# Low halves of two weight blocks per pair: GpSimd subtraction replaced by a ScalarE negation and an accumulating transfer

## The chip, the cores and the metric

The kernel runs on one core of one Trainium2 chip. The metric is the device time of one execution in microseconds (us). The kernel before takes 930.64 us, the median of 3 runs (930.52 to 931.39).

## The reference

One decoder layer over 512 tokens of width 1024, in float32: a SwiGLU feed-forward layer, a mixer (dilated attention beside a diagonal state-space model), and a second SwiGLU layer. Each sub-layer is wrapped in RMS norms and added to the residual.

```
def swiglu(x, w_in, w_out):
    gate, up = jnp.split(x @ w_in, 2, axis=-1)
    return (jax.nn.silu(gate) * up) @ w_out

    h = rms_norm(x, ffn1_pre_g[l])
    x = x + 0.5 * rms_norm(swiglu(h, ffn1_w_in[l], ffn1_w_out[l]), ffn1_post_g[l])
    ...
    h = rms_norm(x, ffn2_pre_g[l])
    x = x + 0.5 * rms_norm(swiglu(h, ffn2_w_in[l], ffn2_w_out[l]), ffn2_post_g[l])
```

`w_in` is 1024 x 5632 (2816 gate and 2816 up columns), `w_out` is 2816 x 1024. The change touches only the two `w_in` products.

## The kernel before

**Split products.** TensorE works on a reduced float32 format (fp32r). To keep float32 accuracy each operand is split into a high half, which is the value rounded to fp32r, and a low half, which is the value minus its high half. A product is then three matmuls: high times high, high times low of the activations, low times high of the weights (`mm3`, lines 136 to 139, and `times`, lines 570 to 577).

**Weights.** A weight block of 128 x 1024 float32 (512 KB) is fetched by a DMA that SyncE issues (`block`, line 559, `load`, line 109). ScalarE writes the high half `whi` (line 105), and VectorE or, where `pool=True`, GpSimd writes the low half `wlo` (line 107). `whi` and `wlo` each have four buffers for the whole kernel, used in rotation. So the cut of a block can begin when TensorE has finished with the block four cuts earlier.

**Pairs.** The first blocks of hidden columns are done in the plain way, eight in the first layer and six in the second. The rest of each `w_in` product is done two column blocks at a time by a scheme of seven block products in place of eight (`seven`, lines 494 to 627). One call of `pair(f)` loads four raw blocks, a11 and a12 (gate columns, tile `wraw`, three buffers) and a21 and a22 (up columns, tile `wx`, three buffers). It forms three sums on VectorE (c3 = a11 + a21, c2 = c3 + a22, c1 = a21 + a22, and later c2 + a12, tile `wsum`), cuts seven blocks into halves (a11, a12, c2, c1, c3, the second c2, a22) and multiplies each with a prepared block of activations, 24 matmuls of 128 x 256 per cut. The sums of products stay in three PSUM banks, X (`wx` in the rows of TensorE), Y (`wy`) and Q (`wq`). ScalarE copies X away twice and Q once in between (`keep`, line 579), since the same bank goes on accumulating in the next product. Of the seven cuts, five have their low half made by VectorE, and two, a12 and a22, by GpSimd.

There are 15 pairs: 7 in the first feed-forward layer (f = 8 to 20) and 8 in the second (f = 6 to 20). Output products `outp` stand between some of them, after f = 12 in the first layer and after f = 10 and f = 16 in the second. So the pairs come in five unbroken runs.

**Order of work.** All matmuls are kept in the order of the program (`fix`, line 123). The instructions of the pairs on ScalarE, VectorE, GpSimd and SyncE have no such order written: a planner places them on each engine by its own costs, and each engine then runs its list in order. A DMA is issued by an engine's queue when its turn comes and its waits are met. No DMA of the kernel before is issued by GpSimd.

Of the kernel before, what the change touches and what calls it, by code (L numbers as in the profile page):

```python
# [8 lines left out]
F32 = mybir.dt.float32  # L9
F32R = mybir.dt.float32r  # L10
I32 = mybir.dt.int32
AF = mybir.ActivationFunctionType
ALU = mybir.AluOpType
# [30 lines left out]
class Layer:  # L44
# [449 lines left out]
    def seven(self, fin, w_in, ig, r, ah, al):  # L494
# [4 lines left out]
        nc, V = self.nc, self.nc.vector  # L499
# [64 lines left out]

        def cut(t, pool=False):
            hi, lo = (self.wp.tile([P, 1024], F32R, name=n, tag=n, bufs=4) for n in ("whi", "wlo"))
            self.wsplit(t, hi, lo, pool)
            return hi, lo

        def times(bank, w, xb, first):  # L570
# [13 lines left out]
        def pair(f, late=False):  # L584
# [5 lines left out]
            X = self.bank("wx")  # L590
            a11 = block(f, 0, 0)
            times(X, cut(a11), b11, True)
            s1 = keep(X)
            a12 = block(f, 0, 1)
            h12 = cut(a12, True)
            Y = self.bank("wy")
            times(Y, h12, b21, True)
# [4 lines left out]
            c2 = wsum()  # L602
            add(c3, a22, c2)
            times(X, cut(c2), n2, False)
            s2 = keep(X)
            c1 = wsum()
# [873 lines left out]
```

## Time and profile before

| | |
|---|---|
| median of 3 runs | 930.64 us |
| the profiled execution | 929.2 us, of which the span from its first to its last instruction is 927.4 us |
| granted TensorE clock | 0.999 of full speed |
| TensorE busy | 99% of the span |
| VectorE, ScalarE, GpSimd busy | 70%, 48%, 23% |
| low halves of a12 and a22 on GpSimd | 30 of GpSimd's 127 instructions |

In the rows, PE is TensorE (PEld its weight loads), DVE is VectorE, ACT is ScalarE, POOL is GpSimd and SP is SyncE. A row of a timeline has the start in us, the duration in us, the engine, the line of the kernel, the operation, and what is written from what, then the idle time before it and what ended that. A row of a tile's view has shortest, median and longest duration in ns, and the first and last start in us.

### The profile page before, as it was taken

What the parts mean: (1) busy time and instruction counts of PE and PEld (TensorE: products, weight loads), DVE (VectorE), ACT (ScalarE), POOL (GpSimd) and SP (SyncE); (2) the same over time, 40 slices, a digit from 0 to 9 for tenths busy, and PEclk for the clock granted to TensorE, in tenths of its full rate; (3) what the DMA queues carried; (4) which work ended last, traced back from release to release, by engine and by line L of the source; (5) the groups of instructions that cost most, each with busy time, mean ns of one, the idle gap of its engine ahead of it and who ended that gap; (6) DMA issues with size and microseconds to landing.
All of it is one profiled execution on the core that took longest, in us unless ns stands there. A gap on an engine that the chain in (4) does not pass through costs nothing.

```text
span 927.4 us, 15348 instructions
## 1 busy us (share of the span) xinstructions
PE 914.6 (99%) x6162; PEld 817.6 (88%) x6162; DVE 650.2 (70%) x1071; ACT 442.6 (48%) x685; POOL 213.7 (23%) x127
## 2 busy tenths in 40 slices
PE   9999999999999999999999999999999999999996
PEld 7887789998999989978777899888899989998995
DVE  6999694755577566758898568698367556755856
ACT  7263764552355443525745654482355414541542
POOL 0433202222223134500000025432122312231321
PEclk9999999999999999999999999999999999999999
DMA  8224652324231162283321440345223322332322
GB/s 274 91 69 139 213 207 90 110 84 132 84 117 44 58 195 90 88 207 122 114 69 56 162 148 24 84 167 182 92 93 113 114 92 94 112 114 93 94 88 90
DMA packets 47590, 106.81 MB, mean 115 GB/s; under 512 B 7808, under 2 KB 11136, under 8 KB 46976
## 3 DMA queue, kind: packets, MB, share of 16 engines
q1 hardware_dynamic: 45936, 102.21, 34.0%
q10 hardware_dynamic: 1584, 3.63, 1.1%
q8 instruction: 48, 0.79, 0.3%
q14 instruction: 22, 0.18, 0.1%
HBM read 96.13 MB, written 9.70 MB: 114 GB/s over the span
## 4 chain that ended last, share of the span: by engine, by line
PE 82%; DVE 3%; DMA 2%; issue 1%; ACT 1%; POOLq 0%; POOL 0%; DVEq 0%; SPq 0%; ACTq 0%
PE yo L132 21%; PE wx L132 18%; PE wq L132 9%; PE yt L132 6%; PE gu L132 5%; PE first L132 5%; PE wy L132 5%; PE prj L132 4%; PE prv L132 2%; PE mo L132 2%; PE st L132 1%; PE ys L132 1%; DMA w1d<-w1s 1%; PE pt L1070 1%; PE sc L132 1%
## 5 line engine op out<-in xcount | busy, mean ns | idle before, releaser
L105 ACT CAST whi<-wraw 128x1024 fp32r<-128x1024 f32 (+5 forms) x129 | 125.1, 977 | 164.3 <-PE yo L132 65.5
L107 POOL TENSOR_TENSOR wlo<-wraw,whi 128x1024 fp32r<-128x1024 f32 (+1 forms) x41 | 109.3, 2665 | 305.0 <-ACT whi L105 297.7
L107 DVE TENSOR_TENSOR wlo<-wraw,whi 128x1024 fp32r<-128x1024 f32 (+5 forms) x88 | 106.9, 1222 | 87.6 <-ACT whi L105 87.4
L132 PE MATMUL wx<-tq,whi 128*128 128x256 f32 x720 | 129.3, 280 | 0.0
L132 PEld LDWEIGHTS wx<-tq,whi 128*128 128x128 f32 x720 | 110.3, 188 | 0.0
L107 DVE TENSOR_TENSOR wlo<-wsum,whi 128x1024 fp32r<-128x1024 f32 x60 | 73.3, 1221 | 46.7 <-ACT whi L105 46.7
L105 ACT CAST whi<-wsum 128x1024 fp32r<-128x1024 f32 x60 | 62.9, 1049 | 90.2 <-PE yo L132 28.0
L132 PE MATMUL wx<-tq,wlo 128*128 128x256 f32 x360 | 100.4, 279 | 0.0
L107 POOL TENSOR_TENSOR wlo<-wx,whi 128x1024 fp32r<-128x1024 f32 x15 | 39.1, 2608 | 185.1 <-ACT whi L105 185.1
L132 PE MATMUL gu<-xh,wlo 128*128 128x512 f32 x176 | 69.0, 392 | 1.9 <-POOL wlo L107 1.2
L132 PE MATMUL gu<-xh,whi 128*128 128x512 f32 x176 | 70.6, 401 | 0.0
L132 PE MATMUL gu<-xl,whi 128*128 128x512 f32 x176 | 68.6, 390 | 0.0
L132 PE MATMUL wq<-bh,wlo 128*128 128x256 f32 x240 | 68.1, 284 | 0.0
L132 PE MATMUL wq<-bh,whi 128*128 128x256 f32 x240 | 68.0, 283 | 0.0
L132 PE MATMUL wq<-bl,whi 128*128 128x256 f32 x240 | 67.9, 283 | 0.0
L132 PEld LDWEIGHTS wx<-tq,wlo 128*128 128x128 f32 x360 | 67.6, 188 | 0.0
L132 PE MATMUL yo<-ah,whi 128*128 128x512 f32 x144 | 56.3, 391 | 0.0
L132 PE MATMUL yo<-whi,ah 128*128 128x512 f32 x144 | 56.1, 389 | 0.0
L132 PE MATMUL yo<-ah,wlo 128*128 128x512 f32 x144 | 56.1, 389 | 0.0
L132 PE MATMUL yo<-al,whi 128*128 128x512 f32 x144 | 56.0, 389 | 0.0
L132 PE MATMUL yo<-whi,al 128*128 128x512 f32 x144 | 56.0, 389 | 0.0
L132 PE MATMUL yo<-wlo,ah 128*128 128x512 f32 x144 | 56.0, 389 | 0.0
(261 smaller groups left out, 2384.8 us busy)
## 6 DMA issues: line engine op xcount, KB each, us to landing
wraw<-w1i SPq DMA_DIRECT2D x28, 512.0 KB, 3.6
wraw<-w2i SPq DMA_DIRECT2D x28, 512.0 KB, 3.6
wraw<-w2o SPq DMA_DIRECT2D x18, 512.0 KB, 3.8
wx<-w2i SPq DMA_DIRECT2D x16, 512.0 KB, 3.7
wx<-w1i SPq DMA_DIRECT2D x14, 512.0 KB, 3.6
wraw<-wmi SPq DMA_DIRECT2D x12, 512.0 KB, 3.8
wraw<-w1o SPq DMA_DIRECT2D x8, 512.0 KB, 4.3
wraw<-w1o SPq DMA_DIRECT2D x8, 384.0 KB, 3.0
```

Of the source, the lines that this page charges most:

```text
L105: fix(self.nc.scalar.copy(out=hi, in_=raw))
L107: fix(eng.tensor_tensor(out=lo, in0=raw, in1=hi.bitcast(F32), op=ALU.subtract))
L132: i = self.nc.tensor.matmul(*a, **k)
L1070: self.fix(nc.tensor.transpose(b[i][:, o:o + P], sc[:, c:c + P], self.ident))
```

## The change

Inside a pair, the two cuts that were made with GpSimd no longer use `wsplit`. ScalarE still writes the high half. ScalarE then also writes the negative of the high half into the low half's buffer, and a transfer issued by GpSimd adds the raw block to what stands there. The value is the same: raw minus high. All other cuts, in the pairs and outside, stay as they are.

```
--- before.py
+++ after.py
@@ -564,7 +564,12 @@

         def cut(t, pool=False):
             hi, lo = (self.wp.tile([P, 1024], F32R, name=n, tag=n, bufs=4) for n in ("whi", "wlo"))
-            self.wsplit(t, hi, lo, pool)
+            if pool:
+                nc.scalar.copy(out=hi, in_=t)
+                nc.scalar.activation(out=lo, in_=hi.bitcast(F32), func=AF.Copy, scale=-1.0)
+                nc.gpsimd.dma_start(out=lo, in_=t, accum_op=ALU.add)
+            else:
+                self.wsplit(t, hi, lo)
             return hi, lo
```

The two calls with `pool=True` are `cut(a12, True)` (line 595) and `cut(a22, True)` (line 617).

## The prediction

> **What bounds the kernel now.** I began with the page, then asked what waits for the 30 low halves that the change moves, and last read one pair on every engine.
>
> ```profile
> span 927.4 us, 15348 instructions
> ...
> PE 914.6 (99%) x6162; PEld 817.6 (88%) x6162; DVE 650.2 (70%) x1071; ACT 442.6 (48%) x685; POOL 213.7 (23%) x127
> ```
>
> TensorE is busy for 914.6 of 927.4 us. Nothing that frees another engine can gain more than the 12.8 us between them, and only where TensorE waits for what is freed. The view of the low halves that GpSimd writes tells whether it does:
>
> ```profile
> L107 POOL TENSOR_TENSOR wlo<-wraw,whi x41: 1844/2406/6822, 24.1 to 893.8; 128x1024 fp32r<-128x1024 f32 x37, 128x768 fp32r<-128x768 f32 x4
> L107 POOL TENSOR_TENSOR wlo<-wx,whi x15: 2427/2437/3061, 159.3 to 888.1; 128x1024 fp32r<-128x1024 f32 x15
> ...
>   ACT whi L105: 482.7, 51
> ...
> who waited for it (us, times):
>   PEld gu L132: 1.6, 1
>   PE gu L132: 1.2, 1
> ```
>
> The waits of TensorE on these tiles are one on a weight load and one on a matmul, both of `gu`, a bank of the plain products. No product of a pair (`wx`, `wy`, `wq`) waited for GpSimd even once. So the change takes nothing off the path. It can only keep the time or add to it, and the question is how much room the new chain has. One pair lasts 20.0 us, and TensorE does not stop in it:
>
> ```profile
> core 0: us, PE busy (x) PEld busy (x) DVE busy (x) ACT busy (x) POOL busy (x), PEclk, DMA share, GB/s
> 169.44:189.46 20.02, 20.02 (x171) 20.02 (x170) 14.85 (x16) 10.74 (x12) 5.42 (x2) 1.00 0.28 92
> ```
>
> **The room.** In the timelines of the first layer's second pair, a22 (`wx`) is cut from 158.13 and a12 of the next pair (`wraw`) from 163.80:
>
> ```profile
> 158.13 1.05 ACT L105 CAST whi<-wx 128x1024 fp32r<-128x1024 f32 x1 [1.78 <-PE wx L132]
> 159.09 0.58 ACT L581 COPY kp<-wx 128x512 f32<-128x512 f32 x1
> 160.97 1.05 ACT L105 CAST whi<-wraw 128x1024 fp32r<-128x1024 f32 x1 [1.30 <-PE wq L132]
> 161.93 0.57 ACT L581 COPY kp<-wq 128x512 f32<-128x512 f32 x1
> 163.80 1.05 ACT L105 CAST whi<-wraw 128x1024 fp32r<-128x1024 f32 x1 [1.30 <-PE wx L132]
> 166.69 1.05 ACT L105 CAST whi<-wsum 128x1024 fp32r<-128x1024 f32 x1 [1.83 <-PE wq L132]
> ```
> ```profile
> 159.26 2.44 POOL L107 TENSOR_TENSOR wlo<-wx,whi 128x1024 fp32r<-128x1024 f32 x1 [17.12 <-ACT whi L105]
> 164.93 2.40 POOL L107 TENSOR_TENSOR wlo<-wraw,whi 128x1024 fp32r<-128x1024 f32 x1 [3.23 <-ACT whi L105]
> ```
> ```profile
> 160.89 0.40 PE L132 MATMUL wx<-tq,whi 128*128 128x256 f32 x2
> ...
> 166.84 0.28 PE L132 MATMUL wx<-tq,wlo 128*128 128x256 f32 x1
> ...
> 172.56 0.28 PE L132 MATMUL wy<-bh,wlo 128*128 128x256 f32 x1
> ```
>
> The high half of a22 is ready at 159.18 and the first matmul with its low half starts at 166.84, 7.66 us later. For a12 it is 164.85 and 172.56, 7.71 us. The distance is set by the four buffers in rotation: a cut begins when TensorE leaves the block four cuts back, and is used three products later. GpSimd needs 2.44 us of it, so some 5.1 us are spare. If a chain lands later than that, TensorE stands still for the difference, and the next cuts shift with it, so a delay is not won back.
>
> How many cuts are so tight? All 15 of a22 start inside a pair. Of the 15 of a12, the first of each of the five unbroken runs of pairs is cut during output products, far ahead (below: written at 139.69, first used at 152.54, 12.85 us later). Ten remain. One a22 is worse off: GpSimd is busy with another split until 870.74, and TensorE wants the block at 875.68.
>
> ```profile
> 139.69 2.44 POOL L107 TENSOR_TENSOR wlo<-wraw,whi 128x1024 fp32r<-128x1024 f32 x1 [30.57 <-ACT whi L105]
> ...
> 870.74 2.43 POOL L107 TENSOR_TENSOR wlo<-wx,whi 128x1024 fp32r<-128x1024 f32 x1
> ```
> ```profile
> 152.54 0.28 PE L132 MATMUL wy<-bh,wlo 128*128 128x256 f32 x1
> ...
> 875.68 0.28 PE L132 MATMUL wx<-tq,wlo 128*128 128x256 f32 x1
> ```
>
> **What goes.** 30 subtractions on GpSimd, 2.4 us each by the rows above (some 73 us). Beside VectorE they run longer, 3.06 us at most in the pairs, and VectorE is slowed too. Neither is on the path: worth 0.
>
> **ScalarE's negation.** 30 activations of 128 x 1024, priced by the nearest row:
>
> ```profile
> L616 ACT ACTIVATE gp<-gp 128x1024 f32<-128x1024 f32 x15 | 15.8, 1056 | 2.9 <-DVE gp L615 2.9
> ```
>
> Two per pair add 2.1 us to ScalarE's 10.74 of 20.02. That is covered by its idle time, but the order counts. After a22's cast stands the copy of bank X (159.09 to 159.67), and TensorE writes X again at 160.89. If the copy goes first, as I take it because it is ready at once, the negation runs from about 159.7 to 160.75; if the negation goes first, it ends at 160.3 and the copy at about 160.85, still just in time. Both leave ScalarE free for its next cast at 160.97. For a12 nothing stands behind the cast until 166.69, so the negation ends at 165.99. A handover between engines takes 0.08 us (159.18 to 159.26), so the transfer can be issued at 160.8 for a22 and 166.07 for a12. TensorE needs it landed about 0.25 us ahead of its matmul (weight load and handover), at 166.6 and 172.3. **The room for the transfer is 5.8 us for a22 (6.2 with the negation first) and 6.2 us for a12.**
>
> **The transfer itself.** No row shows an accumulating transfer, nor one that GpSimd issues. It reads 512 KB of raw block and 512 KB of destination, and writes 512 KB. The nearest rows are a plain load of 512 KB, and moves of 1 MB and of several at once:
>
> ```profile
> L562 SPq DMA_DIRECT2D wx<-w1i x2: 368/368/368, 159.0 to 161.7; - x2
> ...
> DMA to landing us min/median/max: 3.5/3.5/3.5
> ```
> ```profile
> L1015 SPq DMA_DIRECT2D w2d<-zb x2: 328/328/328, 113.9 to 114.8; - x2
> ...
> DMA to landing us min/median/max: 4.3/5.2/6.2
> ```
> ```profile
> L128 SPq DMA_DIRECT2D w<-w2d x4: 582/604/610, 507.5 to 509.4; - x4
> ...
> DMA to landing us min/median/max: 4.7/6.2/7.8
> ```
>
> From below, 3.5 us: it behaves as a plain 512 KB. From above, nothing in the trace bounds it firmly; 7.8 us, the slowest 512 KB here (fourth of four in flight), serves. Alone I take it as a move of 1 MB, 4.3 us, since it has twice the reads. On top comes the making of descriptors in GpSimd's software. Its shortest instruction on a single column per partition stands for that:
>
> ```profile
> L763 POOL TENSOR_TENSOR rs<-sums,mhalf 128x1 f32<-128x1 f32 x4 | 2.6, 658 | 24.0 <-DVE sums L760 24.0
> ```
>
> That gives 4.3 + 0.7 = 5.0 us, with bounds of 0 and 2.4 us (as long as the subtraction it replaces) for the 0.7.
>
> **The collision it makes.** SyncE's queue refills the buffer of a22 as soon as that block is released, now at the end of GpSimd's subtraction (161.70), and another load stands behind it:
>
> ```profile
> 161.72 0.37 SPq L562 DMA_DIRECT2D wx<-w1i  x1
> 163.31 0.37 SPq L562 DMA_DIRECT2D wraw<-w1i  x1
> ```
>
> After the change the raw block is released when the transfer lands, near 166. The first load waits until then with the second queued behind it. Both then run beside the transfer of a12, which is issued at 166.07. The loads themselves have time: the oldest sum that reads them is formed some 10 us later, one pair ahead. But the transfer of a12 gets a share of the DMA engines. Four loads in flight landed 4.7 to 7.8 us after issue, 1.0 us per load ahead. Two loads add 2.0: 7.0 us for a12. The transfer of a22 meets only the tail of the load issued at 159.02, for which I add 0.5: 5.5 us.
>
> **The sum.** a12: (7.0 - 6.2) x 10 = 8 us. a22: 5.5 against 5.8 to 6.2, 14 x 0 = 0. The late a22: 875.68 - 0.25 - 870.74 leaves 4.7 us, 5.5 - 4.7 = 0.8. Negations, removed subtractions, later loads: 0. That is +8.8 us on the profiled execution's 929.2, 938.0; the median of the runs shown stands 1.4 above it, so **939.4 us**. With the nearest bounds for the transfer of a12 (6.2 to 8.0) its own range is 931 to 952.
>
> **Rivals.**
>
> *A, hidden.* The transfer lands within 6 us everywhere. Then only the late a22 can cost, 0 to 1 us, and the time is 931 us. For it: 5.0 us alone, and the engines' DMA share of 0.28 in the pair leaves them idle most of the time. Against: the collision, and a price for software descriptors taken from an instruction of another kind. The Trainium skill speaks for this case: "DMA: Bandwidth & Descriptors" (Anatomy of one DMA) fits a transfer that GpSimd issues as 2.0 us plus bytes at 436 GB/s, and "Collectives: The Full Stack" (The bandwidth ceiling) says that a reducing transfer halves its rate by its two reads and not by its addition. An estimate from both is 2.0 + 2.4 = 4.4 us, by which the sum would be 0; no run here shows it so far, though the plain load's 3.5 us is near the 3.2 us of the fit.
>
> *B, the transfer is far slower than a move of its bytes.* Either the addition in the DMA engines or the writing of descriptors sets the pace. At 9.5 us (4.3 + 2 x 2.4 + 0.4) the cost is 3.3 x 10 + 3.7 x 14 + 4.8, some 90 us, 1020 us; at 8 us it is 18 + 31 + 3, 982 us. For it: GpSimd shares something with VectorE, as this row shows beside a normal 2.44, and VectorE is busy 14.85 us of a pair:
>
> ```profile
> 179.29 3.01 POOL L107 TENSOR_TENSOR wlo<-wx,whi 128x1024 fp32r<-128x1024 f32 x1 [11.95 <-ACT whi L105]
> ```
>
> If descriptors wait in the same way, each transfer waits 0.6 us and more. Against: the two engines lose little even there. The Trainium skill, "SBUF — State Buffer" (Who interferes with whom), names that shared port, and says that only some VectorE operations keep descriptors from being written; the two-input operations of a pair take its read side, so by that page the wait would not come.
>
> *C, on the other side: faster.* Where VectorE is freed from the shared port it finishes earlier, and the planner, with GpSimd's 73 us gone, may order ScalarE better, so that some of the 12.8 us come back. At most 2 to 4 us, 927 us. Against: no wait of a pair ends on these engines.
>
> *D, the planner puts the negation so that bank X is copied late.* 0 to 0.3 us at 14 places, 934 us at most, and only together with a hidden transfer.
>
> **Chances.** The forecast 0.43, A 0.29, B 0.20, C 0.04, D 0.04. What a measurement of this kernel can tell from no change is about 0.2%, 1.9 us. Faster: C and a little of A, 0.05. Same: most of A and half of D, 0.30. Slower: 0.65. The range reaches from A's lower end, 929.5, to the milder part of B, 985.
>
> **What would show it.** In the changed kernel's trace: ScalarE has 30 negations of about 1.05 us, two per pair, and GpSimd no subtraction from line 107 in the pairs. Transfers issued by GpSimd land 5.0 to 5.8 us after issue for a22 and 6.2 to 8 for a12. SyncE's second `wx` load of a pair moves from 3.6 us after the cast of a22 to about 8 us after it. TensorE waits about 0.8 us ahead of the first `wy` matmul with a low half, in ten pairs, and hardly ahead of `wx<-tq,wlo`. A pair then lasts 20.8 us in place of 20.0. I am wrong if the a22 transfer lands after 6.2 us (then both products wait and B's sum holds), if a12 lands as soon as a22 (no collision, then A), or if TensorE waits on ScalarE or VectorE in place of a transfer.

## The result, and the profile after

The changed kernel takes 939.99 us (median; 939.7 to 941.3) against 930.58 us before on the same chip. The ratio is 1.0102, with a 95% interval of 1.0084 to 1.0119. The forecast was 939.4. The profiled execution took 939.7 us, 10.5 more than the one before; its span is 937.9 us.

The page of the changed kernel: the span, the engines, and the new queue.

```profile
span 937.9 us, 15447 instructions
...
PE 916.6 (98%) x6162; PEld 817.6 (87%) x6162; DVE 648.7 (69%) x1071; ACT 473.3 (50%) x715; POOL 165.1 (18%) x127
...
q0 software_dynamic: 4320, 15.73, 9.3%
...
wlo<-wraw POOLq DMA_DIRECT2D x15, 512.0 KB, 5.9
wlo<-wx POOLq DMA_DIRECT2D x15, 512.0 KB, 5.1
```

GpSimd is relieved by 48.6 us: some 75 us of subtractions go, and the issues of the 30 transfers bring 26. ScalarE has 30.7 us more, as planned. What changed for TensorE stands in the view of waits:

```profile
PEld wy L132 <- DMA wlo<-wraw: 5.8, 6, 1.8
...
PEld wx L132 <- DMA wlo<-wx: 2.7, 3, 2.1
```

These waits did not exist before. TensorE waits 5.8 us, in six places, for the transfer of a12, and 2.7 us, in three, for that of a22, one of them of 2.1 us. Measured as longer products the two come to 6.1 and 2.7 us, 8.8 in all. The other 1.7 of the 10.5 us arise outside the pairs: 0.5 before the first pair and 1.1 in the mixer, where TensorE once waits 1.0 us for a load that the change doesn't touch.

One pair in which both parts can be seen, in the timelines of ScalarE, GpSimd, SyncE and TensorE:

```profile
158.67 1.05 ACT L568 CAST whi<-wx 128x1024 fp32r<-128x1024 f32 x1 [1.78 <-PE wx L132]
159.63 0.58 ACT L586 COPY kp<-wx 128x512 f32<-128x512 f32 x1
160.10 1.06 ACT L569 ACTIVATE wlo<-whi 128x1024 fp32r<-128x1024 f32 x1
...
165.43 1.06 ACT L569 ACTIVATE wlo<-whi 128x1024 fp32r<-128x1024 f32 x1
```
```profile
161.47 0.86 POOL L570 DMA_DIRECT2D wlo<-wx  x1 [18.50 <-PE wq L132]
166.78 0.86 POOL L570 DMA_DIRECT2D wlo<-wraw  x1 [4.44 <-ACT wlo L569]
```
```profile
163.85 0.37 SPq L562 DMA_DIRECT2D wraw<-w1i  x1
166.29 0.37 SPq L562 DMA_DIRECT2D wx<-w1i  x1
```
```profile
172.98 0.28 PE L132 MATMUL wy<-bl,whi 128*128 128x256 f32 x1
173.82 0.39 PE L132 MATMUL wy<-bh,wlo 128*128 128x256 f32 x1 [0.56 <-DMA wlo<-wraw]
```

The copy of bank X goes ahead of the negation. The transfer of a22 is issued at 161.47. The refill of a22's buffer, which went out at 161.72 before, now goes out at 166.29, as soon as that transfer has landed. The transfer of a12 is issued at 166.78, half a microsecond later. The view of GpSimd's writes to `wlo`, taken for each of the two transfers by itself:

```profile
DMA to landing us min/median/max: 4.8/4.8/4.8
```
```profile
DMA to landing us min/median/max: 7.0/7.0/7.0
```

The first (a22) lands after 4.8 us, 1.1 us ahead of its use. The second (a12) takes 7.0 us and is 0.7 us late: its matmul would have started at 173.10, 0.12 after the one before, and starts at 173.82. In a pair that no refill follows, the one whose a12 transfer is issued at 302.61, the same transfer takes 4.5 us and nobody waits.

A table by stage of the changed kernel, three pairs from the first `wx` product to the next. A row has the stretch, its length, the busy time and instructions of PE, PEld, DVE, ACT and POOL, then the granted clock, the DMA share and GB/s:

```profile
149.96:169.97 20.01, 20.01 (x169) 20.00 (x168) 12.13 (x12) 12.24 (x14) 1.73 (x2) 1.00 0.46 128
169.97:191.24 21.27, 20.54 (x170) 20.14 (x169) 15.42 (x17) 12.76 (x14) 1.76 (x2) 1.00 0.55 129
191.24:211.25 20.01, 20.01 (x170) 20.01 (x169) 10.96 (x12) 11.24 (x13) 2.71 (x2) 1.00 0.52 138
```

The first and the third pair last 20.01 us as before. The second lasts 21.27: 0.82 of it for its a12 and 0.43 for its a22. The loss is not a tax on each pair, but falls on those where transfers and loads meet. The ten transfers of a12 inside the runs of pairs show it: six met a refill issued between 0.5 us before them and 0.3 us after, and took 6.6 to 8.0 us; two met one issued 0.7 and 0.8 us after them, and took 5.9 and 5.7; one met none and took 4.5; the last, beside the late transfer of a22 and a load of `w2t`, took 5.9. TensorE waited for the first six alone.

### The profile page after: what moved, and what is told of

It is laid out like the page before. It is cut to its first block, busy times and chain, and to the rows that moved or that the text cites. A ratio compares the mean times of both kernels' runs of the same rounds, so it can differ in the third digit from the quotient of the medians.

```text
span 937.9 us, 15447 instructions
## 1 busy us (share of the span) xinstructions
PE 916.6 (98%) x6162; PEld 817.6 (87%) x6162; DVE 648.7 (69%) x1071; ACT 473.3 (50%) x715; POOL 165.1 (18%) x127
## 4 chain that ended last, share of the span: by engine, by line
PE 74%; DMA 9%; DVE 3%; issue 2%; ACT 1%; POOLq 0%; SPq 0%; POOL 0%; DVEq 0%; ACTq 0%
PE yo L132 21%; PE wx L132 13%; PE wq L132 7%; PE yt L132 6%; PE gu L132 5%; PE first L132 5%; DMA wlo<-wraw 5%; PE wy L132 4%; PE prj L132 4%; PE prv L132 2%; DMA wlo<-wx 2%; PE st L132 1%; PE mo L132 1%; DMA w1d<-w1s 1%; PE gl L132 1%
## 5 line engine op out<-in xcount | busy, mean ns | idle before, releaser
L105 ACT CAST whi<-wraw 128x1024 fp32r<-128x1024 f32 (+5 forms) x114 | 109.5, 969 | 115.8 <-PE yo L132 49.5
L107 DVE TENSOR_TENSOR wlo<-wraw,whi 128x1024 fp32r<-128x1024 f32 (+5 forms) x88 | 102.2, 1167 | 89.5 <-ACT whi L105 89.3
L132 PE MATMUL wx<-tq,whi 128*128 128x256 f32 x720 | 129.3, 280 | 0.0
L132 PEld LDWEIGHTS wx<-tq,whi 128*128 128x128 f32 x720 | 110.2, 188 | 0.0
L107 POOL TENSOR_TENSOR wlo<-wraw,whi 128x1024 fp32r<-128x1024 f32 (+1 forms) x26 | 73.4, 2822 | 203.5 <-ACT whi L105 196.1
L132 PE MATMUL wx<-tq,wlo 128*128 128x256 f32 x360 | 100.7, 280 | 2.1 <-DMA wlo<-wx 2.1
L132 PE MATMUL gu<-xh,wlo 128*128 128x512 f32 x176 | 69.0, 392 | 2.0 <-POOL wlo L107 1.2
L132 PE MATMUL gu<-xh,whi 128*128 128x512 f32 x176 | 70.5, 401 | 0.0
L132 PEld LDWEIGHTS wx<-tq,wlo 128*128 128x128 f32 x360 | 67.6, 188 | 2.7 <-DMA wlo<-wx 2.7
L132 PE MATMUL gu<-xl,whi 128*128 128x512 f32 x176 | 68.6, 390 | 0.0
L132 PE MATMUL wq<-bh,wlo 128*128 128x256 f32 x240 | 68.1, 284 | 0.0
L132 PE MATMUL wq<-bh,whi 128*128 128x256 f32 x240 | 68.0, 283 | 0.0
L132 PE MATMUL wq<-bl,whi 128*128 128x256 f32 x240 | 67.9, 283 | 0.0
L132 PE MATMUL yo<-ah,whi 128*128 128x512 f32 x144 | 56.3, 391 | 0.0
L132 PE MATMUL yo<-whi,ah 128*128 128x512 f32 x144 | 56.1, 389 | 0.0
L132 PE MATMUL yo<-ah,wlo 128*128 128x512 f32 x144 | 56.1, 389 | 0.0
L132 PE MATMUL yo<-al,whi 128*128 128x512 f32 x144 | 56.0, 389 | 0.0
L132 PE MATMUL yo<-whi,al 128*128 128x512 f32 x144 | 56.0, 389 | 0.0
L132 PE MATMUL yo<-wlo,ah 128*128 128x512 f32 x144 | 56.0, 389 | 0.0
L570 POOL DMA_DIRECT2D wlo<-wx x15 | 13.0, 869 | 218.7 <-PE wq L132 218.7
```

The lines of the kernel that those rows point to most:

```text
L105: fix(self.nc.scalar.copy(out=hi, in_=raw))
L107: fix(eng.tensor_tensor(out=lo, in0=raw, in1=hi.bitcast(F32), op=ALU.subtract))
L132: i = self.nc.tensor.matmul(*a, **k)
L570: nc.gpsimd.dma_start(out=lo, in_=t, accum_op=ALU.add)
```

## The experiments

The theory: the transfer of a12 is late because the refill of a22's buffer, held back by a22's own transfer, runs beside it. The rivals: the transfer is slow of itself; ScalarE's additional work costs the time; GpSimd's software sets the pace.

**One part alone: a12.** a22's low half is made by GpSimd's subtraction again.

```
     def cut(t, pool=False):
         ...
-                self.wsplit(t, hi, lo)
+                self.wsplit(t, hi, lo, pool is None)
 ...
-            times(X, cut(a22, True), t4, False)
+            times(X, cut(a22, None), t4, False)
```

> Only a12 goes through the accumulating transfer; the low half of a22 is made by GpSimd's subtraction again. Theory (a12 lands late because the refill of a22's buffer, held back by a22's own transfer, runs beside it): the second wx load of a pair goes out some 3.2 us after the cast of a22 starts, as before, the transfers of a12 land within 6.0 us, TensorE waits less than 0.7 us in all ahead of wy matmuls, and the time is 930.6 to 932.5 us. Rival (the transfer of a12 is slow of itself, or through VectorE or the wraw load that is there anyway): 6.6 to 8 us in the same five or six pairs, 6 us of waits, 936.5 to 938.5 us.

930.79 us against 930.64, a ratio of 1.0005 (0.9996 to 1.0014): no change. The view of GpSimd's writes to `wlo` in the pairs, and SyncE's timeline in the pair shown above:

```profile
L570 POOL DMA_DIRECT2D wlo<-wraw x14: 874/877/941, 166.2 to 876.5; - x14
...
DMA to landing us min/median/max: 4.5/4.6/5.5
```
```profile
158.91 3.12 SPq L562 DMA_DIRECT2D wx<-w1i  x2
163.26 0.37 SPq L562 DMA_DIRECT2D wraw<-w1i  x1
```

The refill is back at 161.7 (the second of the first row), and no transfer takes longer than 5.5 us, though the load of `wraw` still runs beside the first 1.5 us of the transfer. No matmul waits for one. So the accumulating transfer of a12 is not slow of itself, and the rival falls.

**The other part alone: a22.** The same edit with `cut(a12, None)` and `cut(a22, True)`.

> Only a22 goes through the accumulating transfer; the low half of a12 is made by GpSimd's subtraction again. Theory: the transfers of a22 land as in the changed kernel (4.8 to 6.2 us, the late one near the end 7.0), the refill is held back but meets no transfer of a12, TensorE waits 2 to 3 us ahead of wx<-tq,wlo and nothing ahead of wy, 933 to 935 us. Rival (both transfers are slow for a common reason, and the waits only fell on a12 by chance of order): a22 lands after 6.5 us in most pairs, 937 us or more.

934.21 us, a ratio of 1.0052 (1.0036 to 1.0068), as the theory had it. TensorE waits in four places ahead of `wx`, 3.1 us in all, and nowhere ahead of `wy`:

```profile
PEld wx L132 <- DMA wlo<-wx: 3.1, 4, 1.6
```

Alone, the parts cost 0.2 and 3.6 us by their medians; together 9.4. So 5.6 us arise only where both are present. By the ratios it is nearer 4.2 us, since two of the six executions with a22 alone took 937.5 us. Either way the two together cost more than their sum.

**The collision made by hand.** To the kernel with a12 alone, which lost nothing, one move of 512 KB is added beside the transfer. It writes a high half to memory that nobody reads (the line that reserves that memory is left out here).

```
                 nc.gpsimd.dma_start(out=lo, in_=t, accum_op=ALU.add)
+                nc.scalar.dma_start(out=self.side, in_=hi.bitcast(F32))
```

> As the kernel in which only a12 goes through the accumulating transfer (it had no wait and the time of before), with one move more: right behind the issue of a12's transfer, ScalarE's queue stores the 512 KB of a12's high half to a scratch in device memory, that nobody reads. Theory (one move of 512 KB beside the transfer is what makes it late): the transfers of a12 in the pairs land after 5.8 to 7.5 us in place of 4.5 to 5.5, TensorE waits 2 to 8 us in all ahead of wy, 933 to 939 us. Rival (the refill was not the cause; a22's own transfer just ahead of it was): a12 still lands within 5.5 us, 930 to 932 us.

937.84 us, a ratio of 1.0086 (1.0072 to 1.0100), with no transfer of a22 in the kernel. The view of GpSimd's writes to `wlo` in the pairs (this kernel has one line more above them, so L571 and L133 are the L570 and L132 of the others):

```profile
L571 POOL DMA_DIRECT2D wlo<-wraw x14: 874/877/941, 167.1 to 883.8; - x14
...
  PEld wy L133: 6.3, 6
...
DMA to landing us min/median/max: 4.6/5.7/8.0
```

The longest transfer grows from 5.5 to 8.0 us, and TensorE waits 6.3 us in six places, as in the changed kernel. The transfer is still issued 0.3 us after the negation ends, as without the store, so the store doesn't work by delaying its start. The store itself does not stand behind the transfer, as I had meant it to, but goes out 1.4 us ahead of it, when the high half is ready.

The store is not the only thing that differs. At four of the six places where TensorE waits, two loads of `wx` go out later than in the kernel without the store (at the longest transfer 3.6 and 3.2 us ahead of it, there 6.3 and 4.1). At the other two the loads stand as they stood. The first of these is the pair shown above, where the same view of this one transfer gives, without the store and with it:

```profile
DMA to landing us min/median/max: 4.7/4.7/4.7
```
```profile
  PEld wy L133: 1.3, 1
...
DMA to landing us min/median/max: 7.5/7.5/7.5
```

So a move beside the transfer and the load of `wraw` is enough to make it late. At four places the store alone ran beside it and had landed 1.3 us after its issue; there the transfer took 4.6 to 5.0 us. How much of the 6.3 us the later loads add is not shown.

**The negation alone.**

```
                 nc.scalar.activation(out=lo, in_=hi.bitcast(F32), func=AF.Copy, scale=-1.0)
-                nc.gpsimd.dma_start(out=lo, in_=t, accum_op=ALU.add)
```

> ScalarE's negation stays and the transfer is left out, so that the low halves of a12 and a22 hold the negative high half: the sums of these products are not the reference's. Theory: no wait of TensorE in the pairs, and 930.6 to 932.3 us; what stands above 930.6 is the share of the planner's other order and of ScalarE. Rival (ScalarE's additional 2.1 us per pair, or the late copy of bank X, is a part of the loss): TensorE waits on ScalarE, 933 us or more.

931.03 us, a ratio of 1.0007 (0.9998 to 1.0015). ScalarE's 30 instructions are covered by its idle time.

**The transfer without the addition.**

```
-                nc.gpsimd.dma_start(out=lo, in_=t, accum_op=ALU.add)
+                nc.gpsimd.dma_start(out=lo, in_=t)
```

> GpSimd issues the same transfer without the addition, so that the low halves of a12 and a22 hold the raw block: the sums of these products are not the reference's. Theory (an accumulating transfer costs as much as a move of 1 MB, by its second read): the copy lands 0.5 to 1 us sooner than the accumulating one (3.8 to 4.3 us alone against 4.5 to 5.4, up to 6 beside loads against 8), TensorE waits less than 1.5 us in all, 931 to 933 us. Rival (the issue by GpSimd's software and the fixed part set the length, the second read costs nothing): 4.5 to 5 us alone, 938 to 940 us.

931.92 us, a ratio of 1.0014 (1.0005 to 1.0023), within what the theory gave. The view of GpSimd's writes to `wlo` in the pairs:

```profile
L570 POOL DMA_DIRECT2D wlo<-wx x15: 527/530/567, 161.6 to 893.0; - x15
...
  PEld wx L132: 0.8, 1
...
DMA to landing us min/median/max: 2.9/4.3/6.1
```

Alone the copy lands after 2.9 us where the accumulating transfer takes 4.5: the addition, with its second read, costs 1.6 us, twice what I had expected of it here. It is 1.5 to 1.8 at four of the five places with no load beside them; at the fifth (759.76) both take 5.4 us, and the cause of that is open. GpSimd is busy 0.53 us with its issue and 0.87 with the accumulating one. Beside loads the copy too takes up to 6.1 us, but that is still inside the room. One wait is left, of the late a22.

**No load of a22.** a21's block serves for both, so that the buffers of `wx` turn over half as fast.

```
-            a21, a22 = block(f, 1, 0), block(f, 1, 1)
+            a21 = a22 = block(f, 1, 0)
```

> Both transfers stay, but a22 is not loaded: a21's block is used for both (so the products with a22 are not the reference's), and one up block per pair rotates through the three buffers, so that no load has to wait for a transfer's end. Theory (the refill held back by a22's transfer is what slows a12's): no wx load goes out at the landing of a22's transfer, the transfers of a12 land within 5.7 us, waits ahead of wy below 1 us in all against 6 in the changed kernel, 931 to 934.5 us. Rival (the two transfers disturb one another, or a12's is slowed by the wraw loads): a12 still lands after 6.6 us in several pairs, 936.5 us or more.

938.35 us (934.0 to 938.92), a ratio of 1.0075 (1.0060 to 1.0091), and the theory's numbers were missed. The experiment did not take away what it was to take away, as SyncE's timeline shows:

```profile
163.12 0.37 SPq L562 DMA_DIRECT2D wraw<-w1i  x1
165.58 0.37 SPq L562 DMA_DIRECT2D wx<-w1i  x1
```

SyncE issues a load whenever a buffer comes free, however early the block is wanted. The one `wx` load that is left in a pair again goes out at the landing of a22's transfer (issued 160.75, 4.8 us). So the collision stayed: that pair's a12 transfer takes 7.4 us. The profiled execution is the fastest of the six, though, at 934.0 us, and TensorE waits less in it than in the changed kernel:

```profile
PEld wx L132 <- DMA wlo<-wx: 2.9, 2, 2.5
...
PEld wy L132 <- DMA wlo<-wraw: 1.4, 2, 1.1
```

The waits for a12 are 1.4 us in place of 5.8, and most of the rest is the late a22. Where the executions around 938 us lose some 4 us more, no trace here shows. So the run decides nothing between theory and rival; that role fell to the store made by hand.

**Two halves.** The transfer is cut into two of 512 columns.

```
-                nc.gpsimd.dma_start(out=lo, in_=t, accum_op=ALU.add)
+                for h in range(2):
+                    c = slice(h * S, (h + 1) * S)
+                    nc.gpsimd.dma_start(out=lo[:, c], in_=t[:, c], accum_op=ALU.add)
```

> The accumulating transfer is issued as two, of 512 columns each: the first 12 matmuls of a product use only the first, the others come 1.4 us later. Theory (bytes beside other loads set the length): the first half lands 1 to 2 us sooner than the whole does now, waits of TensorE in the pairs fall from 8.8 to below 3 us, 931.5 to 934.5 us. Rival (a fixed part and GpSimd's making of descriptors set it): the first half lands hardly sooner, the second 1 us later than the whole, 939 us or more.

934.89 us, a ratio of 1.0052 (1.0040 to 1.0064), a little above the theory's range and far below the rival's. The waits come to 3.7 us, where less than 3 was expected. The waits by TensorE:

```profile
PEld wx L132 <- DMA wlo<-wx: 3.1, 3, 1.5
...
PEld wy L132 <- DMA wlo<-wraw: 0.6, 2, 0.4
```

The waits for a12 fall from 5.8 to 0.6 us, those for a22 stay. In the pair shown, a22's first half lands 3.3 us after its issue, against 4.8 for the whole transfer. The second half costs something: issued 0.5 us behind the first, it lands 5.3 us after its own issue.

**Twice the transfer.** The same transfer is issued a second time behind the first.

```
                 nc.gpsimd.dma_start(out=lo, in_=t, accum_op=ALU.add)
+                nc.gpsimd.dma_start(out=lo, in_=t, accum_op=ALU.add)
```

> Two accumulating transfers in a row into each of the 30 low halves, the second after the first has landed (the low halves get one raw block too many and the sums are not the reference's). It tests the rule by which the forecast was priced: room 5.8 us for a22 and 6.2 for a12, and each us beyond it stops TensorE for 1 us, never won back. By the rule, with 10.0 us for a22 and 10 to 12 us for a12: 14 x 4.2 + 10 x 4.8 + 5 or so, some 110 us, 1030 to 1065 us, and a pair of 29 to 30 us. Rival (a later cut is partly won back by the rotation of buffers): below 1010 us.

1037.21 us in its one execution, inside the range that the rule gave. But its parts are others, so that the hit is luck. TensorE's waits:

```profile
PEld wx L132 <- DMA wlo<-wx: 70.2, 15, 7.2
...
PEld wy L132 <- DMA wlo<-wraw: 3.6, 3, 2.0
```

a22 waits at all 15 places, a12 hardly at all: while TensorE waits for a22, a12's chain, which has already begun, goes on and gains that time. So waits of cuts that overlap do not add up, and there the rule was wrong. The waits come to 73.8 us, the time grew by some 107, all of it in the products of the pairs. A part of the rest is the clock. Stretches of this kernel around one wait, in the same columns:

```profile
166.30:170.40 4.10, 0.41 (x4) 0.20 (x2) 3.62 (x4) 2.00 (x2) 1.28 (x2) 0.98 0.89 174
170.50:174.70 4.20, 4.20 (x23) 4.20 (x24) 0.00 (x0) 0.01 (x1) 0.86 (x1) 0.62 0.91 217
174.70:178.00 3.30, 3.18 (x27) 2.98 (x25) 2.92 (x3) 2.42 (x3) 0.00 (x0) 1.00 0.86 166
```

After a wait of some 4 us the clock is granted at 0.62 for some 4 us. The product that should last 2.99 us and waited 3.8 us lasted 8.46.

**VectorE for all.** No transfer and no GpSimd: `cut(a12)` and `cut(a22)` without `pool`, in the kernel before.

> No transfer and no GpSimd: VectorE makes the low halves of a12 and a22 as well. It tests the term that freeing GpSimd is worth nothing. Theory: VectorE has 5 us idle in a pair and 2.5 us more to do, no product waits, 930 to 931.5 us. Rival (GpSimd or the port it shares with VectorE holds TensorE up somewhere): faster than 929 us; or VectorE becomes late, over 932 us.

930.79 us against 930.08, a ratio of 1.0001 (0.9992 to 1.0010). GpSimd's subtractions are worth nothing to the time, neither as work to be taken off nor as a relief of VectorE.

## Why the prediction was right

**What goes is worth 0.** Right: with the subtractions on VectorE the time is the same, and with the negation in their place as well.

**ScalarE's negation.** Right in its price (1.06 us) and its place. The copy of bank X goes first; no matmul waits on ScalarE in a pair. The handover was mis-sized: 0.3 us between the negation's end and the issue, not 0.08.

**The room.** 5.8 and 6.2 us were forecast. The rows give 5.9 for a22 (161.47 to 167.38, where its first low product starts on time) and 6.3 for a12 (166.78 to 173.1). The forecast's 0.25 us between landing and matmul was too much: the a12 transfer above lands at 173.78 and its matmul starts at 173.82.

**The transfer alone.** 5.0 us forecast, 4.5 to 5.4 measured. Its two terms were both wrong in size and made up for one another: a bare GpSimd transfer takes 2.9 us and not 3.5 + 0.7, and the second read and addition 1.6 us and not 0.8. The estimate from the Trainium skill in rival A, 2.0 + 2.4 = 4.4 us ("DMA: Bandwidth & Descriptors", Anatomy of one DMA, with "Collectives: The Full Stack", The bandwidth ceiling), agrees with the 4.5 us; its plain 3.2 us stand against 2.9. Where it was taken to lead, to rival A, it did not: A fell by the collision, which no price of a lone transfer holds.

**The collision.** The mechanism is shown, by taking either part away and by making it by hand. 7.0 us were forecast for a12; 6.6 to 8.0 were measured where TensorE waited. One detail was wrong: the `wraw` load does not stand behind the refill. The planner put it ahead (163.85, 166.29), and alone it does no harm. So what was priced as two loads behind one another was one refill and the end of a load, and these added 2.1 to 3.5 us to the lone 4.5, where 2.0 had been added to 5.0. The 7.0 is right by two errors that made up for one another.

**The sum.** 8.8 us forecast in the pairs, 8.8 measured, with other parts: a12 6.1 in place of 8, since six of the ten met a refill in full and not ten. a22 0.7 in place of 0 at two ordinary places, where its transfer took 6.0 and 6.2 us beside loads. The late a22 2.1 in place of 0.8: its transfer of 7.0 us runs beside two loads of `w2t` that I had not looked for. The 1.4 us added for the median stood in for the 1.7 us outside the pairs: the profiled execution after is 0.3 us under its median. So much of the precision of 939.4 against 939.99 is luck. The upper end of the forecast's own range does not come out of its terms either: with 8.0 us for a12 they give 949.4, not 952.

**Rivals.** B fell: no accumulating transfer takes over 8 us, and none waits for VectorE in a way that the rows show. With no loads beside them they take 4.5 to 5.5 us, VectorE busy or not: in the kernel with a12 alone the one issued at 299.25 takes 4.5 with VectorE busy for 4.2 of them, and the one at 665.99 takes 5.0 with 1.0. That is in line with what "SBUF — State Buffer" (Who interferes with whom) of the Trainium skill says of two-input operations; no run here tries the other kind. Nothing pointed to C or D. The sign that was to point to B, a22 landing after more than 6.2 us, came once, in the late a22 with 7.0, and cost that one wait and not B's sum.

**Not settled.** What the loss of the kernel with one `wx` load is made of, and the 1.7 us outside the pairs. The profile of the kernel with the negation alone stands 3.0 us of span above that of before, with no wait in its pairs, while its median is 0.4 us above. So a single profile scatters by more than 1.7 us there, and I put these to no cause.

## What to carry to other kernels

Price a transfer put on a path by what runs beside it, not alone: ask which buffer it holds longer than the engine did, which load waits for that buffer, and what is in flight when that load goes out. Here the transfer of one block sent a load into the transfer of the next, which cost more than both alone. And where the bounding engine never waits for the work that is moved, expect nothing from moving it: here GpSimd's subtractions could go to VectorE with a ratio of 1.0001, and the view of who waited for them had pointed to it before any experiment.

## What the runs showed of the hardware

An accumulating transfer of 512 KB within SBUF, issued by GpSimd, lands 4.5 to 5.5 us after its issue when alone and up to 8.0 us beside loads. A plain copy issued the same way lands after 2.9 to 3.2 at four of five places where it is alone, and after 5.4 at the fifth. The issue takes GpSimd 0.87 and 0.53 us.

A wait of TensorE costs more than its length when it is long: after 4 us of idleness the clock was granted at 0.62 for some 4 us. The Trainium skill ("TensorE: Matmul & The Clock Gate", Part 1) says so: after about 3.4 us of idleness the array starts again at half rate, for about as long. The stretches above agree. I had not used it for the price of a long wait in rival B. After the 2.1 us of the late a22 in the changed kernel it stayed at 1.00:

```profile
883.80:886.10 2.30, 0.44 (x4) 0.24 (x2) 1.79 (x2) 2.00 (x2) 0.66 (x1) 1.00 1.04 296
886.10:889.00 2.90, 2.87 (x25) 2.87 (x26) 1.93 (x4) 0.18 (x1) 0.00 (x0) 1.00 1.01 222
```
